# Next quad's branch announced before this quad's gather; x copied in the gather's column order; extra code of one pass and a loop

## The chip, the cores and the metric

The kernel runs on one core of a Trainium2 chip. The metric is the device time of one execution in microseconds (us); the kernel before has a median of 1836.73 us in three runs, from 1834.0 to 1844.76. TensorE (PE) multiplies matrices; its weight loads are listed as PEld. VectorE is DVE, ScalarE is ACT, GpSimd is POOL, and SyncE (SP) issues most DMA transfers. A "q" behind an engine's name (PEq, PEldq) means its sequencer.

## The reference

The reference is a network of two blocks on 256 tokens with 1024 features, all in fp32. The first block has two layers, each of a mixer of four attentions, a cross attention to a memory, and a mixture of experts (MoE), with a layer norm behind each. The second block (four layers of pooling, neighbourhood attention and convolution) is not touched. The change lies in the MoE:

```
def one_sequence(xs):
    g_logits = (xs @ w_group + b_group).astype(jnp.float32)
    g_idx = jnp.argmax(g_logits, axis=-1)
    ...
    e_logits = e_logits[jnp.arange(s), g_idx]
    top_val, top_idx = lax.top_k(e_logits, TOP_K_IN_GROUP)
    top_w = jax.nn.softmax(top_val, axis=-1) * g_weight
    ...
    hid = jax.nn.silu(jnp.einsum('sd,edf->sef', xs, w_gate)) * jnp.einsum('sd,edf->sef', xs, w_up)
    return jnp.einsum('sef,efd->sd', hid * gates[:, :, None], w_down)
```

There are 32 experts in 8 groups of 4. A token goes to one group and to two experts in it. An expert has a gate and an up matrix (1024 x 256 each) and a down matrix (256 x 1024), so each is 1 MiB.

## The kernel before

The program is written by a class `Net`. Its parts are coroutines that a planner, `Flow`, interleaves; the order of the instructions on each engine is thus fixed when the program is written. `moe(l)` writes the MoE of layer l (0 or 1). It walks over eight **quads** q, one per group of four experts. An expert has 32 places for tokens, so a quad has 128 places in one pass. If more than 32 tokens choose one expert, the quad takes further passes; their number, `more`, is known only at run time, and stands in a register.

The x of a layer (two tiles of 128 tokens x 1024) is written by `ln_affine` (L1104 multiplies by the gain, L1105 adds the bias, in place). For each tile the four pieces of 512 columns are shared between POOL (tile 0) and DVE (tile 1). DVE does the router's small operations behind that, from L1322 on.

For quad q the steps on PE are these:

- `gather` (the product at L1400): x is multiplied by the one-hot matrix `disp` to collect the quad's tokens, transposed. The weights that PE loads are columns k, k+8, k+16, ... of x, with k from 0 to 7, thus 128 columns at a stride of 8 elements. One gather is 16 products in fp32; the trace shows each as two loads and two matmuls, so one gather is 32 of each. `disp` is the name in the trace for the main pass; in the extra passes, and in the first gather of a layer, it is named `y`.
- `gate_up`: 128 rows in the trace `ps<-w,xg` with the expert weights that SP has loaded.
- The branch `up{l}_{q}` (L1533): if `more > 1`, the code of the extra passes runs (dispatch, gather, gate_up); otherwise PE jumps over it. Two passes are written out (the second behind a test at L1536), and from the fourth pass on a loop runs (L1538 and L1539).
- The gather of quad q+1, the matrices of `combine_mats`, and `down` with the quad's down weights into `acc`.
- The branch `down{l}_{q}` (L1584), with extra passes in the same form (tests at L1587 and L1589).

Two hints (`mark_branch_hint_location`, in the trace `BRANCH_PREFETCH_HINT` of L2345, on PE alone) name a branch ahead of time. The hint for `down{l}_{q}` stands right behind the up extras, and the hint for `up{l}_{q+1}` right behind the down extras, just ahead of the gate_up of quad q+1. The hint for quad 0 stands in front of the first gather.

At the end of the layer L1608 computes `x * ALPHA + acc` on DVE in four pieces.

Of the kernel before, what the change touches and what calls it, by code (L numbers as in the profile page):

```python
# [14 lines left out]
OP = mybir.AluOpType  # L15
AX = mybir.AxisListType

P = 128
# [5 lines left out]
ALPHA = 4.0 ** 0.25  # L24
# [111 lines left out]
class Net:  # L136
# [958 lines left out]

        self.flow.spawn(gen(), 0)

    def ln_affine(self, rows, eng=None):

        for tb in range(2):  # L1100
            for nh in range(2):
                e = eng[2 * tb + nh] if eng else self.nc.gpsimd
                x = self.x[tb][:, nh * 512:nh * 512 + 512]
                e.tensor_tensor(x, x, rows[0][nh], OP.mult)  # L1104
                e.tensor_tensor(x, x, rows[1][nh], OP.add)  # L1105

    def trans_bank(self, xs, j):

# [197 lines left out]
    def router(self, l, wr, rb):  # L1306

        nc = self.nc
        xf = [self.M2("xf32") for _ in range(4)]
        yield 0, 4.0  # L1310
        for j in range(4):
            self.affine_t(xf[j], self.trans_bank(self.halves(self.x), j), j,
                          lambda k: self.col("ln_mem_g", 8 * l + k), lambda k: self.col("ln_mem_b", 8 * l + k))
            yield 0.6, 0
        self.ln_affine(self.rows, (nc.gpsimd, nc.gpsimd, nc.vector, nc.vector))
        yield 0, 0.8
        p = self.ps()
        for tb in range(2):
# [25 lines left out]
        p = self.ps()  # L1344
# [47 lines left out]
    def gather(self, d, xg):  # L1392

        res = []
        dv = d.rearrange("p t e s -> p t (e s)")
        for k0 in range(0, 8, 4):
            p = self.ps()
            for j in range(4):
                for tb in range(2):
                    self.mm(p[:, j * P:(j + 1) * P], self.x[tb][:, k0 + j::8], dv[:, tb, :], tb == 0 and j == 0, tb == 1)  # L1400
            t = xg[k0 // 4].rearrange("p (k s) -> p k s", k=4)
            if k0:
                self.nc.vector.tensor_copy(xg[1], p)  # L1403
            else:
                self.nc.scalar.copy(xg[0], p)
            res += [t[:, j, :] for j in range(4)]
        return res
# [68 lines left out]
    def moe(self, l):  # L1476
        nc, tc = self.nc, self.tc
# [7 lines left out]
        hx = self.e("hx", [P, EXTRA * 256])  # L1485
# [3 lines left out]
        h, h2 = self.places()  # L1489
# [3 lines left out]
        mores = nc.values_load_multi_w_load_instructions(nri[0:1, :], min_val=0, max_val=8)[1]  # L1493
        pe = [mybir.EngineType.PE]
# [18 lines left out]
        for q in range(8):  # L1513
            if q == 1 and l == 0:
                prep = self.flow.spawn(self.band(), 0)
            wg = [self.raw("E", "expert_w_gate", l, 4 * q + j, 8) for j in range(4)]
            wu = [self.raw("E", "expert_w_up", l, 4 * q + j, 8) for j in range(4)]
            gv, uv = [w for w, _ in wg], [w for w, _ in wu]
            more = mores[q]
            rk = self.s("rk", [P, 2, 4], bufs=1)  # L1520
            if q:
                h, h2 = self.places()

            def extra_up(out):
                nc.vector.tensor_scalar(rk, rk, -32.0, None, OP.add)
                self.gate_up(self.gather(self.dispatch(rk, onehot(h2)), [self.y(0), self.y(1)]), gv, uv, out)

            gates = gates or rest()
            now, d0 = comb, d
            if q < 7:  # L1530
                d = self.dispatch(rank[:, :, 4 * q + 4:4 * q + 8])
            self.gate_up(xg, gv, uv, h)
            with tc.If(more > 1, label=f"up{l}_{q}"):  # L1533
                nc.vector.tensor_copy(rk, rank[:, :, 4 * q:4 * q + 4])
                extra_up(hx[:, 0:256])
                with tc.If(more > 2):  # L1536
                    extra_up(hx[:, 256:512])
                    with tc.If(more > 3):  # L1538
                        with tc.For_i(3, more) as i:  # L1539
                            extra_up(h2)  # L1540
                            nc.vector.tensor_copy(hx[:, self.at(i)], h2)
            tc.mark_branch_hint_location(f"down{l}_{q}", more > 1, pe)
            for _, i in wg + wu:
                self.used(i)
            if q == 3:
                self.far.close()
                if l:
                    self.near.close()
                    assert self.plan is None or not self.live_p
                self.other(split=SPLITS, more=MORE[l])  # L1550
                if l:
                    self.perm, self.capp = self.near.enter_context(self.tc.tile_pool(name="late", bufs=LATE, reuse_waits="tile", side="right")), LATE
                self.keep, self.stage = True, 2 * l + 1
                self.n_split = SPLITS
                self.pump()
                main.lane = "ps"
            yield 8.5, 0
            yield from between(3 * q)
            if q < 7:
                xg = self.gather(d, xt)  # L1560
                now = now or self.combine_mats(flat(d0), gates[:, :, 0, :])
                comb = self.combine_mats(flat(d), gates[:, :, q + 1, :])
                ht = self.down_in(h)
                yield 5.0, 0 if q > 2 else 3.0
                yield from between(3 * q + 1)
            else:
                ht = self.down_in(h)
            if q == 7 and not l:
                self.adas.append(self.flow.spawn(self.ada(1), 2, 6.0))
            gq = gates[:, :, q, :]  # L1570
            wd = [self.raw("E", "expert_w_down", l, 4 * q + j, 2) for j in range(4)]
            dv = [w for w, _ in wd]

            def extra_down(h, src=None):
                dx, h2 = self.places()
                if h is None:
                    h = h2
                    nc.vector.tensor_copy(h, src)
                nc.vector.tensor_scalar(rk, rk, -32.0, None, OP.add)
                d2 = self.dispatch(rk, onehot(dx))  # L1580
                self.down(self.down_in(h), dv, *self.combine_mats(flat(d2), gq, "x"))

            def extras():
                with tc.If(more > 1, label=f"down{l}_{q}"):  # L1584
                    nc.vector.tensor_copy(rk, rank[:, :, 4 * q:4 * q + 4])
                    extra_down(hx[:, 0:256])
                    with tc.If(more > 2):  # L1587
                        extra_down(hx[:, 256:512])
                        with tc.If(more > 3):  # L1589
                            with tc.For_i(3, more) as i:  # L1590
                                extra_down(None, hx[:, self.at(i)])

            self.down(ht, dv, *now, q == 0)
            extras()
            if q < 7:
                tc.mark_branch_hint_location(f"up{l}_{q + 1}", mores[q + 1] > 1, pe)
            if q == 7:
                nc.scalar.preload_act_table_set("natural_log_exp_and_others")
            for _, i in wd:
                self.used(i)  # L1600
            if q == 7:
                self._ahead()
            if q == 7:
                st = [self.s("bn", [P, 2, 6], bufs=2) for _ in range(2)]
                for half in range(2):
                    for tb in range(2):
                        x = self.x[tb][:, half * 512:half * 512 + 512]
                        nc.vector.scalar_tensor_tensor(x, x, ALPHA, self.acc[tb][half], OP.mult, OP.add)  # L1608
                        self.bn_half(st, half, tb)
            yield 6.0, 0 if q > 2 else 10.0  # L1610
            yield from between(3 * q + 2)
            if q == 2 and l == 0:
                yield prep.done
# [530 lines left out]
    def layer_b(self, l):  # L2144

        with ExitStack() as ctx:
            self.phase(ctx, 6)
            self.stage = 2 * l
            self.other(ring2=RING2)
            self.exp = ctx.enter_context(self.tc.tile_pool(name="exp", bufs=1, reuse_waits="tile"))  # L2150
            self.y = lambda i, dt=F32: self.e(f"y{i}", [P, 512], dt)
            self.rows = [[], []]
            for i in range(4):
                t, c = self.y(i), i % 2 * 512
                self.nc.sync.dma_start(t, self.a["ln_mem" + ("_g", "_b")[i // 2]][l:l + 1, c:c + 512].to_broadcast([P, 512]))
                self.rows[i // 2].append(t)
            self.wr = self.router_weights(l)
            self.pump()
            yield from self.moe(l)

# [188 lines left out]
```

## Time and profile before

| | |
|---|---|
| median of 3 runs | 1836.73 us |
| profiled execution, its own time | 1837.78 us |
| its span, first to last instruction | 1836.0 us |
| mean granted clock of TensorE | 0.947 of full speed |
| PE busy | 1649.1 us, 90% |
| DVE busy | 918.4 us, 50% |
| MoE of layer 0, of layer 1 | from about 306 to 602 us, from 876 to 1250 us |

The page of the profile lists busy times and the chain of work that ended last; the grouped list says how long instructions of one kind took; the timeline shows them in order; the view of one source line shows a branch's wait on each engine's sequencer; the table of windows shows how busy the DMA engines were in a stretch.

### The profile page before, as it was taken

The page shows a single profiled execution, that of the slowest core. Times are in us where ns is not written, and L with a number is a line of the kernel's source. Part 1 is how long each engine was busy: PE and PEld are TensorE (multiplying, and loading weights), DVE is VectorE, ACT ScalarE, POOL GpSimd, SP SyncE. Part 2 cuts the span into 40 slices and gives each one's busy share as a digit, 9 for nine tenths or more (in the row PEclk, how much of TensorE's full clock was granted, in tenths as well). Part 3 has the DMA queues.
Part 4 walks back from the last instruction along what each step waited for, and adds up shares of the span by engine and source line. Part 5 has one row for each costly group of instructions (what it writes and reads, how often), then busy time and mean ns, then how long its engine had stood idle before and what let it go on. Part 6 is the DMA issues. An engine that isn't in the chain of part 4 may idle for free. (4 is left out here: it accounts for less than half of the span.)

```text
span 1836.0 us, 29061 instructions
## 1 busy us (share of the span) xinstructions
PE 1649.1 (90%) x11357; PEld 1297.9 (71%) x11357; DVE 918.4 (50%) x2160; ACT 701.1 (38%) x1422; POOL 165.9 (9%) x248
## 2 busy tenths in 40 slices
PE   7999997788888799988898898997998999899997
PEld 6767985556765466686656675866887886699785
DVE  5567545252112756766121243247555566576645
ACT  4654540102212355442010132234545565455543
POOL 4000201000000300031000000002001112000101
PEclk9999998899999899999899999998998999999999
DMA  8266557989957955576357497897456866385630
GB/s 306 85 204 229 187 206 302 389 327 416 364 197 310 385 164 183 184 285 255 129 223 329 168 412 301 317 364 280 139 188 135 207 97 84 121 293 171 235 111 24
DMA packets 145964, 427.29 MB, mean 233 GB/s; under 512 B 12252, under 2 KB 19652, under 8 KB 121172
## 3 DMA queue, kind: packets, MB, share of 16 engines
q1 hardware_dynamic: 140660, 411.19, 60.6%
q0 software_dynamic: 5088, 13.32, 5.3%
q8 instruction: 124, 2.03, 0.5%
q14 instruction: 92, 0.75, 0.1%
HBM read 423.43 MB, written 1.05 MB: 231 GB/s over the span
## 5 line engine op out<-in xcount | busy, mean ns | idle before, releaser
L308 DVE TENSOR_TENSOR wlo<-w,whi 128x512 fp32r<-128x512 f32 (+2 forms) x586 | 395.4, 709 | 265.0 <-ACT whi L307 262.8
L307 ACT CAST whi<-w 128x512 fp32r<-128x512 f32 (+2 forms) x592 | 341.5, 611 | 249.6 <-PE ps L366 199.1
L366 PE MATMUL ps<-xth,whi 128*128 128x256 f32 x896 | 263.9, 295 | 8.7 <-ACT whi L307 5.2
L366 PE MATMUL ps<-xth,wlo 128*128 128x256 f32 x896 | 259.3, 289 | 4.4 <-DVE wlo L308 4.4
L366 PE MATMUL ps<-xtl,whi 128*128 128x256 f32 x896 | 258.5, 289 | 0.6 <-DVE xtl L1142 0.4
L366 PE MATMUL ps<-whi,xth 128*128 128x512 f32 (+2 forms) x512 | 206.6, 404 | 4.4 <-ACT whi L307 4.0
L366 PE MATMUL ps<-wlo,xth 128*128 128x512 f32 (+2 forms) x512 | 198.8, 388 | 0.2 <-DVE wlo L308 0.2
L366 PE MATMUL ps<-whi,xtl 128*128 128x512 f32 (+2 forms) x512 | 198.6, 388 | 0.2 <-DVE xtl L1142 0.2
L366 PEld LDWEIGHTS ps<-xth,whi 128*128 128x128 f32 x896 | 176.0, 196 | 18.1 <-ACT whi L307 12.8
L366 PEld LDWEIGHTS ps<-xth,wlo 128*128 128x128 f32 x896 | 174.8, 195 | 5.2 <-DVE wlo L308 5.2
L366 PEld LDWEIGHTS ps<-xtl,whi 128*128 128x128 f32 x896 | 175.2, 196 | 3.2 <-issue 1.4
L366 PEld LDWEIGHTS ps<-whi,xth 128*128 128x128 f32 x512 | 99.0, 193 | 33.2 <-ACT whi L307 6.6
L366 PEld LDWEIGHTS ps<-whi,xtl 128*128 128x128 f32 x512 | 98.4, 192 | 20.7 <-DVE xtl L1142 0.9
L366 PEld LDWEIGHTS ps<-wlo,xth 128*128 128x128 f32 x512 | 98.9, 193 | 18.3 <-DVE wlo L308 1.3
L366 PE MATMUL ps<-disp,x 128*128 128x128 f32 x384 | 94.4, 414 | 15.7 <-PEq L1533 6.8
L366 PEld LDWEIGHTS ps<-disp,x 128*128 128x128 f32 x384 | 93.0, 336 | 19.0 <-issue 14.3
L366 PE MATMUL ps<-w,xg 128*32 128x256 f32 x1536 | 86.9, 382 | 6.1 <-issue 2.8
L366 PE MATMUL ps<-w,y 128*32 128x512 f32 (+1 forms) x784 | 80.9, 551 | 6.9 <-DVE y L1451 4.4
L366 PEld LDWEIGHTS ps<-w,xg 128*32 128x32 f32 x1536 | 52.1, 111 | 40.2 <-issue 7.3
L1142 POOL TENSOR_TENSOR xtl<-aff,xth 128x512 fp32r<-128x512 f32 x9 | 11.6, 1285 | 696.9 <-ACT xth L1141 521.5
L1403 DVE COPY xg<-ps 128x512 f32<-128x512 f32 x14 | 9.7, 692 | 118.9 <-PE ps L366 118.9
L1435 DVE TENSOR_TENSOR y<-y,ps 128x256 f32<-128x256 f32 x12 | 5.1, 421 | 112.6 <-ACTq L1533 62.9
(516 smaller groups left out, 2567.0 us busy)
## 6 DMA issues: line engine op xcount, KB each, us to landing
w<-in_expert_w_gate_dram SPq DMA_DIRECT2D x64, 1024.0 KB, 14.4
w<-in_expert_w_up_dram SPq DMA_DIRECT2D x64, 1024.0 KB, 12.6
w<-in_expert_w_down_dram SPq DMA_DIRECT2D x64, 1024.0 KB, 10.0
w<-in_ada_w_dram SPq DMA_DIRECT2D x48, 1024.0 KB, 6.1
w<-in_pool_w_in_dram SPq DMA_DIRECT2D x24, 1024.0 KB, 10.9
w<-in_na_w_in_dram SPq DMA_DIRECT2D x24, 1024.0 KB, 6.5
w<-in_w_in_dram SPq DMA_DIRECT2D x16, 1024.0 KB, 11.5
w<-in_conv_w_in_dram SPq DMA_DIRECT2D x16, 1024.0 KB, 6.0
```

What stands on the lines that cost most here:

```text
L307: self.nc.scalar.copy(hi, src)
L308: (self.nc.gpsimd if self.spare and k % 2 else self.nc.vector).tensor_tensor(lo, src, hi.bitcast(F32), OP.subtract)
L366: self.nc.tensor.matmul(out, lhsT, rhs, start=start, stop=stop, skip_group_check=True)
L1142: (nc.gpsimd if j == 2 else nc.vector).tensor_tensor(lo, fs[j - 1], hi.bitcast(F32), OP.subtract)
L1403: self.nc.vector.tensor_copy(xg[1], p)
L1435: nc.vector.tensor_tensor(h, sg, p[:, 256:512], OP.mult)
```

## The change

- `ln_affine` writes the sum of L1104's product and the bias to two further tiles, `xp`, of [128, 8, 128]: `xp[:, k, j]` is column 8j + k of x. For this the second operation reads x and the bias in order and writes with the order turned round. `x` itself then holds only the product.
- `gather` loads `xp[tb][:, k0 + j, :]`, 128 columns that lie next to each other.
- L1608 reads `xp` in the turned order and writes x in plain order.
- The hint for `up{l}_{q+1}` stands right behind the up extras of quad q, so the gather of quad q+1, the `down` of quad q and the branch of its down extras lie between it and the branch it names. The hint for `down{l}_{q}` is dropped. The hint for quad 0 stays.
- Of the extra passes one is written out; from the third pass on (`more > 2`) the loop runs.
- The scratch space for POOL's DMA descriptors is set to 8192.

```
-    def ln_affine(self, rows, eng=None):
+    def ln_affine(self, rows, eng=None, xp=None):
...
                 e.tensor_tensor(x, x, rows[0][nh], OP.mult)
-                e.tensor_tensor(x, x, rows[1][nh], OP.add)
+                o, b = x, rows[1][nh]
+                if xp:
+                    o = xp[tb].rearrange("p k j -> p j k")[:, nh * 64:nh * 64 + 64, :]
+                    x, b = (v.rearrange("p (j k) -> p j k", k=8) for v in (x, b))
+                e.tensor_tensor(o, x, b, OP.add)
...
-                    self.mm(p[:, j * P:(j + 1) * P], self.x[tb][:, k0 + j::8], dv[:, tb, :], tb == 0 and j == 0, tb == 1)
+                    self.mm(p[:, j * P:(j + 1) * P], self.xp[tb][:, k0 + j, :], dv[:, tb, :], tb == 0 and j == 0, tb == 1)
...
                 extra_up(hx[:, 0:256])
                 with tc.If(more > 2):
-                    extra_up(hx[:, 256:512])
-                    with tc.If(more > 3):
-                        with tc.For_i(3, more) as i:
-                            extra_up(h2)
-                            nc.vector.tensor_copy(hx[:, self.at(i)], h2)
-            tc.mark_branch_hint_location(f"down{l}_{q}", more > 1, pe)
+                    with tc.For_i(2, more) as i:
+                        extra_up(h2)
+                        nc.vector.tensor_copy(hx[:, self.at(i)], h2)
+            if q < 7:
+                tc.mark_branch_hint_location(f"up{l}_{q + 1}", mores[q + 1] > 1, pe)
...
-                with tc.If(more > 1, label=f"down{l}_{q}"):
+                with tc.If(more > 1):
                     nc.vector.tensor_copy(rk, rank[:, :, 4 * q:4 * q + 4])
                     extra_down(hx[:, 0:256])
                     with tc.If(more > 2):
-                        extra_down(hx[:, 256:512])
-                        with tc.If(more > 3):
-                            with tc.For_i(3, more) as i:
-                                extra_down(None, hx[:, self.at(i)])
+                        with tc.For_i(2, more) as i:
+                            extra_down(None, hx[:, self.at(i)])
...
-            if q < 7:
-                tc.mark_branch_hint_location(f"up{l}_{q + 1}", mores[q + 1] > 1, pe)
...
-                        x = self.x[tb][:, half * 512:half * 512 + 512]
-                        nc.vector.scalar_tensor_tensor(x, x, ALPHA, self.acc[tb][half], OP.mult, OP.add)
+                        x = self.x[tb][:, half * 512:half * 512 + 512].rearrange("p (j k) -> p j k", k=8)
+                        xp = self.xp[tb].rearrange("p k j -> p j k")[:, half * 64:half * 64 + 64, :]
+                        acc = self.acc[tb][half].rearrange("p (j k) -> p j k", k=8)
+                        nc.vector.scalar_tensor_tensor(x, xp, ALPHA, acc, OP.mult, OP.add)
...
+            self.xp = [self.e(f"xp{tb}", [P, 8, P]) for tb in range(2)]
...
-    nc = _bacc.Bacc("TRN2", target_bir_lowering=False, num_devices=1)
+    nc = _bacc.Bacc("TRN2", target_bir_lowering=False, num_devices=1, dynamic_dma_scratch_size=8192)
```

The changed program numbers its lines a little higher: the up branch L1533 becomes L1537, its inner test L1536 becomes L1540, the loop L1541; the down branch L1584 becomes L1587, its inner test L1590; L1105 becomes L1109, L1608 becomes L1609.

The order of PE's instructions moves at two places of each quad. The first is the end of quad 0's up extras in layer 0, where PE comes out of the branch and begins the gather of quad 1. Before:

```order
L1536 UNCONDITIONAL_BRANCH
L1533 UNCONDITIONAL_BRANCH
L1542 REGISTER_ALU
L2345 BRANCH_PREFETCH_HINT
L366 MATMUL ps<-disp,x 128x128 x8
L366 MATMUL pl<-disp,x 128x128 x8
L369 MATMUL ps<-ident,y_3124 128x128 x2
```

The hint of L2345 here names the down branch of the same quad. With the change, at the same place:

```order
L1540 UNCONDITIONAL_BRANCH
L1537 UNCONDITIONAL_BRANCH
L1545 REGISTER_ALU
L2347 BRANCH_PREFETCH_HINT
L366 MATMUL pl<-disp,xp_2966 128x128
L366 MATMUL pl<-disp,xp_2967 128x128
```

The hint now names the up branch of quad 1, and the gather's weights come from `xp` (the last two rows stand four times in turn for each of `pl` and `ps`).

The second place is the end of quad 0's down extras, where the gate_up of quad 1 begins. Before:

```order
L1589 UNCONDITIONAL_BRANCH
L1587 UNCONDITIONAL_BRANCH
L1584 UNCONDITIONAL_BRANCH
L1596 REGISTER_ALU
L2345 BRANCH_PREFETCH_HINT
L366 MATMUL pl<-w_2974,xg 32x256
```

The hint here names the up branch of quad 1, which stands behind this gate_up. With the change:

```order
L1591 UNCONDITIONAL_BRANCH
L1590 UNCONDITIONAL_BRANCH
L1587 UNCONDITIONAL_BRANCH
L366 MATMUL ps<-w_2976,xg 32x256
L366 MATMUL ps<-w_2978,xg 32x256
```

No hint stands there any more. Counted in the instructions that the trace shows (two loads and two matmuls per product), an up branch before jumped over 994 PE instructions and now over 670, a down branch over 321 and now over 222, and the inner up test L1536 over 674.

## Rows read from the trace of the kernel before

**Rows 1.** The page: chain of work that ended last, share of the span by engine.

```profile
PE 25%; DVE 3%; ACT 1%; DMA 1%; issue 1%; POOL 0%; ACTq 0%; DVEq 0%; POOLq 0%
```

**Rows 2.** Grouped list, 285 to 1250 us: count | busy us, mean ns | idle before.

```profile
L366 PEld LDWEIGHTS ps<-disp,x 128*128 128x128 f32 x384 | 93.0, 336 | 19.0 <-issue 14.3 <-ACTq L1533 4.6
...
L366 PEld LDWEIGHTS ps<-y,x 128*128 128x128 f32 x112 | 27.2, 335 | 8.3 <-issue 8.3
...
L366 PEld LDWEIGHTS pl<-y,x 128*128 128x128 f32 x80 | 19.5, 335 | 6.6 <-issue 6.6
...
L366 PEld LDWEIGHTS pl<-disp,x 128*128 128x128 f32 x64 | 15.7, 334 | 10.0 <-issue 6.8 <-ACTq L1533 1.6 <-ACTq L1538 1.6
...
L366 PEld LDWEIGHTS ps<-wr,xf 128*128 128x128 f32 x64 | 7.3, 192 | 0.0
...
L366 PEld LDWEIGHTS pl<-band,pu 128*128 128x128 f32 x48 | 5.6, 191 | 1.7 <-issue 1.7
```

**Rows 3.** Timeline, 318 to 345 us: the gather of quad 1 (start, length, engine).

```profile
323.47 3.88 PEld L366 LDWEIGHTS ps<-disp,x 128*128 128x128 f32 x16 [2.89 <-ACTq L1533]
...
327.25 3.94 PEld L366 LDWEIGHTS pl<-disp,x 128*128 128x128 f32 x16
```

**Rows 4.** Table of windows; last columns: PE clock, DMA busy share, GB/s.

```profile
310.00:330.00 20.00, 17.56 (x173) 14.41 (x173) 3.21 (x15) 3.61 (x9) 0.00 (x0) 0.87 0.68 263
...
390.00:410.00 20.00, 16.62 (x189) 10.70 (x187) 4.99 (x17) 2.13 (x4) 0.54 (x1) 0.99 0.66 244
410.00:460.00 50.00, 44.32 (x344) 36.03 (x344) 12.48 (x25) 10.28 (x19) 0.00 (x0) 0.90 1.01 411
...
890.00:930.00 40.00, 34.34 (x361) 27.27 (x350) 3.97 (x12) 3.60 (x6) 0.00 (x0) 0.91 0.08 29
...
1000.00:1050.00 50.00, 41.85 (x409) 29.21 (x409) 10.54 (x38) 8.76 (x20) 0.00 (x0) 0.94 0.32 118
1050.00:1110.00 60.00, 57.66 (x444) 46.85 (x446) 19.52 (x36) 20.14 (x37) 3.36 (x5) 0.98 1.02 406
```

**Rows 5.** Timeline of PE: gate_up of layer 0 quad 4, layer 1 quad 1.

```profile
429.20 7.39 PE L366 MATMUL ps<-w,xg 128*32 128x256 f32 x128
...
958.60 7.11 PE L366 MATMUL ps<-w,xg 128*32 128x256 f32 x128 [0.73 <-PEq L1589]
```

**Rows 6.** View of L1533 (up branch), PE's sequencer, six stretches: ns min/median/max.

```profile
L1533 PEldq COMPARE_BRANCH  x3: 1678/2604/5817, 319.6 to 381.1; - x3
...
L1533 PEldq COMPARE_BRANCH  x2: 2812/3125/3438, 405.8 to 434.9; - x2
...
L1533 PEldq COMPARE_BRANCH  x3: 89/4453/4938, 474.1 to 587.0; - x3
...
L1533 PEldq COMPARE_BRANCH  x3: 89/89/967, 889.9 to 992.1; - x3
...
L1533 PEldq COMPARE_BRANCH  x2: 739/2148/3557, 1043.5 to 1082.9; - x2
...
L1533 PEldq COMPARE_BRANCH  x3: 359/1699/2221, 1132.4 to 1232.3; - x3
```

**Rows 7.** Views of L1536 and L1587 (inner tests, no hint), PE's sequencer.

```profile
L1536 PEldq COMPARE_BRANCH  x5: 75/197/3404, 542.0 to 1012.5; - x5
...
L1587 PEldq COMPARE_BRANCH  x5: 65/187/349, 579.7 to 1037.3; - x5
```

**Rows 8.** Views of L2345 (hints), 1150 to 1198 us, and L1533, 1190 to 1198 us.

```profile
L2345 PEldq BRANCH_PREFETCH_HINT  x2: 35/35/35, 1174.0 to 1196.3; - x2
...
L1533 PEldq COMPARE_BRANCH  x1: 1699/1699/1699, 1194.3 to 1194.3; - x1
```

**Rows 9.** Timeline of DVE, 283 to 316 us: adds at L1105 (start, length).

```profile
293.74 1.64 DVE L1105 TENSOR_TENSOR x<-x,y 128x512 f32<-128x512 f32 x1
...
297.08 0.69 DVE L1105 TENSOR_TENSOR x<-x,y 128x512 f32<-128x512 f32 x1
```

**Rows 10.** Grouped list, 285 to 1250 us: L1608.

```profile
L1608 DVE SCALAR_TENSOR_TENSOR x<-x,acc 128x512 f32<-128x512 f32 x4 | 2.7, 674 | 1.1 <-PEq L1584 1.1
```

More of the change, by code (lines that the diff above doesn't have):

```diff
@@ L1314, in router @@
             yield 0.6, 0
-        self.ln_affine(self.rows, (nc.gpsimd, nc.gpsimd, nc.vector, nc.vector))
+        self.ln_affine(self.rows, (nc.gpsimd, nc.gpsimd, nc.vector, nc.vector), self.xp)
         yield 0, 0.8
```

## The prediction

> **What bounds the kernel now.** I read the page first. In the chain that ended last PE holds 25% of the span and no other engine more than 3% [rows 1], and PE is busy for 90% of the span; so time taken off PE is time won, unless what PE works on comes too late. The grouped list then shows what the touched steps cost on PE, and that the rows of one shape differ by a factor of two [rows 2]. The timeline shows that a gather is bounded by its weight loads, which follow each other without a hole [rows 3]. The table of windows tells where the expert weights already come as fast as the DMA engines move them [rows 4], and the timeline of PE where PE uses them as they land [rows 5]. The views of the branches give the waits on PE's sequencer [rows 6 to 8]. The sum is made against the profiled execution, 1837.8 us, which is 1.05 us above the median.
>
> **1. The gather's loads: -80.5 us.** The four groups with x as weights hold 384 + 112 + 80 + 64 = 640 loads and 93.0 + 27.2 + 19.5 + 15.7 = 155.4 us [rows 2]: 243 ns for each load. A gather has 32, so these are 20 gathers: 16 main ones and 4 in extra passes. One of them runs from 323.47 to 331.19 us, 7.7 us for 32 loads [rows 3]. The same shape, 128x128 fp32, taken from columns that lie side by side, costs 7.3 / 64 = 114 ns (`ps<-wr,xf`) and 5.6 / 48 = 117 ns (`pl<-band,pu`) [rows 2]. With `xp` the gather's columns lie side by side, so I take 117 ns: 640 x 0.117 = 74.9 us, 80.5 less, or 4.0 us for each gather. PE goes from the gather to `down` to the next gate_up with little idle time, so all of it is on the path. The Trainium skill ("SBUF — State Buffer", section on the DMA port swizzle, its note on cachelines) says that accesses are at full speed only if at least two fall into one line of 16 bytes, which a stride of 8 fp32 misses; for the loads the rows agree, and the sum is the same by either.
>
> **2. What the weights give back: +14 us.** PE can gain only what the transfers allow. In layer 0 the DMA engines are busy at 1.01 from 410 to 460 us, and in this stretch the gate_up of quad 4 takes 7.39 us where another takes 7.11 [rows 4, 5]: there the weights land as they are used. Five gathers lie ahead of that place, 5 x 4.0 = 20 us. To come 20 us earlier the transfers have only the free shares of two holes, 0.32 x 20 = 6.4 us at 310 to 330 and 0.34 x 20 = 6.8 us at 390 to 410 [rows 4], 13.2 us at most. So 6.8 us are lost if both close fully and 20 if neither does; I take 10, nearer to the first, because the holes come from buffers that come free late, and PE will free them earlier. In layer 1 the shares are 0.08 at 890 to 930 us and 0.32 at 1000 to 1050 [rows 4]: 36.8 + 34 us free, more than its 11 gathers x 4.0 = 44 us. Only the stretch from 1050 us at 1.02 is full, with one gather at its beginning: 4 us. The sum is 14. Bounds: 0, and 40 if all of layer 0's nine gathers (36 us) and this one are lost.
>
> **3. Up branches: -10 us.** Thirteen of the 16 up branches are taken, and the six rows hold their waits: 10.1 + 6.25 + 9.4 + 1.0 + 4.3 + 4.3 = 35.3 us [rows 6] (the three that go on into an extra pass wait 0.09). If the earlier hint hides all but the shortest of these, 0.36 us, 13 x 0.36 = 4.7 stays: -30.6. Against that stands the branch at 1194.3 us: its hint came at 1174.0, 20.3 us ahead, and PE still waited 1.70 us [rows 8]. So lead alone is not enough, and the other bound is 0. I take a third of the way: eight of the thirteen waits are longer than this 1.70 us, by 16.2 us in sum, and of that I count 10 as won. A wait that gets longer is a rival below.
>
> **4. Down branches without a hint: 0 us.** The inner test L1587 skips about as many instructions as the down branch will (some 220), has no hint, and waits 0.35 us at most [rows 7]. That is no more than a hinted down branch costs.
>
> **5. One pass and a loop: +6 us.** Four extra ups and downs run. Quad 0 of layer 1 has three passes and goes through the loop once in up and once in down where it had straight code. The loop adds a copy and two jumps on each side. Lower bound 1 us (two short copies). Above: two misses as long as the longest up wait, 5.8 each [rows 6], and a few us of loop code, 15 us. I take two misses near 3 us, as the unhinted L1536 has at most 3.4 [rows 7]. The two quads with two passes still test and skip the second; 670 instructions less one body make this no dearer.
>
> **6. Turned writes and reads: +4 us.** The adds that now write `xp` stand on DVE ahead of the router's operations, and they took 1.64 and 0.69 us [rows 9]; L1608 takes four times 0.67 us per layer [rows 10] with the next norm behind it. No row shows fp32 written at a stride of 512 bytes. If nothing changes it is 0; if DVE slows down by the factor of the weight loads (243 / 117 = 2.1) it is about 1.1 x (2.33 + 2.7) x 2 layers = 11 us. I take 4, since a slower DVE pays at the short adds, but those of 1.64 us are already held up by POOL, and may hide part. POOL's adds have room before the first gather. Beside this: by the Trainium skill's note named in step 1 the stride of 512 bytes also misses the line; an estimate by it is the upper end, 7 us more than in my sum. No run here shows it yet.
>
> **7. The smaller scratch: 0 us.** POOL issues few transfers in this kernel, and none of them is on the path.
>
> **Sum.** -80.5 + 14 - 10 + 6 + 4 = -66.5: 1837.8 - 66.5 = 1771.3 for a profiled execution, 1770 on the scale of the median.
>
> **The rivals.**
> - **B, all branches hidden (0.20).** The hint a quad ahead hides the up waits: term 3 becomes -30.6, the others stay: 1837.8 - 87.1 = 1750.7, about 1750. For it: the waits are longest where transfers are full, as if the fetch only came too late. Against it: the 20 us of rows 8.
> - **C, the weights become the bound (0.14).** Term 2 is 40: 1837.8 - 40.5 = 1797.3, about 1796. For it: the stretch from 410 to 460 us is full already [rows 4]. Against it: layer 1 has holes of more than 70 us.
> - **D, slower: the hint is lost and branches miss (0.05).** Between the hint and its branch stands another taken branch, the down branch. If that one uses up the hint or drives the fetched code out, and itself misses, 13 up and 13 down branches wait as the worst now, 5.8 us [rows 6]: 26 x 5.8 = 151 us in place of 35.3 and about 7 for the downs, +109. With the other terms (-56.5) that is 1837.8 + 52 = 1890. It ends on the slow side when the mean of the 26 waits is above (42 + 56.5) / 26 = 3.8 us. Against it: unhinted tests wait 3.4 us for 674 instructions and 0.35 for some 220 [rows 7], which would make 13 x 3.4 + 13 x 0.35 = 49 us, +7, and a time near 1787. The Trainium skill ("Runtime: NRT & Kernel Launch", section "Instruction fetch mechanics") says that a taken branch whose target is not in the current window of two pages (256 instructions each) waits for a fetch. By it the up skip of 670 misses without a hint and the down skip of 222 mostly does not; rows 7 agree in kind.
> - **E, the copy does nothing for the loads (0.03).** If the loads of a gather are slow for another reason than their stride (both matmul operands of the quick rows differ too), -80.5 and +14 fall away: 1837.8 + 0 = about 1837. Against it: four groups at 335 ns each and two at 191 of the same shape [rows 2].
>
> **How the numbers follow.** My forecast has 0.58, B 0.20, C 0.14, D 0.05, E 0.03. The predicted time is 1770. A change of under 0.5% (9 us) is about what a measurement of this kernel can't tell from none. Forecast, B and C are faster by more: 0.92; E is the same: 0.03; D is slower: 0.05. The range reaches from B with a little less given back by the weights (1750 less 10) to C and a little above: 1740 to 1800. D and E stay outside, and some of the edges of B and C, together less than 2 in 10.
>
> **What would show it.** The loads of `xp` at 110 to 125 ns each (their duration near 190 in place of 335), a gather in about 3.8 us; the up branch's waits between 5 and 35 us in sum, and the down branch's at 0.2 to 0.5 us each; the gate_ups of layer 0 from quad 3 on with idle time that ends on a DMA of expert weights, 10 us or so; L1609 and L1109 with a mean between 0.67 and 1.4 us. The prediction is wrong if the loads stay above 200 ns, if up waits grow beyond 50 us, or if PE waits for weights for more than 30 us.

## The result, and the profile after

The changed kernel takes 1785.21 us (median of 4 runs, 1781.82 to 1790.64) against 1840.74 us of the kernel before in the same comparison: ratio 0.9703, 95% interval 0.9656 to 0.9749. It is 55.5 us faster, where 66.5 were predicted, and lies inside the range (1740 to 1800). The total was nearly right; several of its terms were not: one had the wrong sign, and one counted a gain that is not there.

The page of the profile after (busy time by engine; chain by engine):

```profile
PE 1590.7 (89%) x11357; PEld 1234.5 (69%) x11357; DVE 926.4 (52%) x2162; ACT 702.5 (39%) x1422; POOL 165.2 (9%) x248
...
PE 23%; DVE 4%; DMA 3%; ACT 1%; issue 1%; POOL 1%; ACTq 0%; DVEq 0%; POOLq 0%
```

PE lost 58 us of busy time, and its count of matmuls is the same as before, 11357: the same products run, in the same order. So the k-th weight load of one trace can be set beside the k-th of the other, and the difference of their starts shows where time was won. Up to the last gate_up of layer 1 these differences add up to 64.7 us won in the 20 gathers, 8.7 lost in the gate_ups with the up branches behind them, and 6.5 lost in all the rest; 2.4 more are lost after it. That makes 47 us, the difference of the two spans (1836.0 and 1788.8 us).

The grouped list after, 285 to 1250 us, answers to [rows 2, 10]:

```profile
L366 PEld LDWEIGHTS ps<-disp,xp 128*128 128x128 f32 x384 | 49.0, 209 | 23.3 <-issue 20.0 <-ACTq L1540 1.6 <-ACTq L1537 1.6
...
L366 PEld LDWEIGHTS ps<-y,xp 128*128 128x128 f32 x112 | 16.8, 239 | 8.3 <-issue 8.3
...
L366 PEld LDWEIGHTS pl<-y,xp 128*128 128x128 f32 x80 | 10.9, 219 | 6.9 <-issue 6.9
L366 PEld LDWEIGHTS pl<-disp,xp 128*128 128x128 f32 x64 | 10.5, 254 | 11.0 <-issue 8.1 <-ACTq L1537 2.9
...
L1609 DVE SCALAR_TENSOR_TENSOR x<-xp,acc 128x512 f32<-128x512 f32 x8 | 8.4, 1045 | 1.1 <-PEq L1587 1.1
...
L1109 DVE TENSOR_TENSOR xp<-x,y 128x512 f32<-128x512 f32 x4 | 6.0, 1506 | 0.1
```

The 640 loads are busy for 49.0 + 16.8 + 10.9 + 10.5 = 87.2 us, 136 ns each, where 117 were predicted. The final multiply-add takes 1.05 us against 0.67 [rows 10], the add 1.51 against a mean of 1.16 before (4.7 us for four in the same list); the prediction had named 0.67 to 1.4 for both.

Why 136 and not 117 shows when the gathers are put beside the granted clock. The timeline of weight loads before, and the table of windows before (last three columns: PE clock, DMA share, GB/s):

```profile
306.11 3.91 PEld L366 LDWEIGHTS ps<-y,x 128*128 128x128 f32 x16 [2.73 <-issue]
...
356.43 1.26 PEld L366 LDWEIGHTS pl<-disp,x 128*128 128x128 f32 x5 [1.49 <-issue]
...
383.92 3.88 PEld L366 LDWEIGHTS pl<-disp,x 128*128 128x128 f32 x16 [1.65 <-ACTq L1533]
```
```profile
306.00:310.00 4.00, 3.86 (x16) 3.90 (x17) 0.00 (x0) 0.00 (x0) 0.54 (x2) 0.50 1.05 424
...
384.00:387.70 3.70, 3.70 (x16) 3.70 (x16) 2.83 (x10) 0.00 (x0) 1.42 (x5) 0.90 0.96 372
```

The same two views after:

```profile
310.76 1.87 PEld L366 LDWEIGHTS pl<-y,xp 128*128 128x128 f32 x16
...
352.43 0.71 PEld L366 LDWEIGHTS pl<-disp,xp 128*128 128x128 f32 x3 [2.54 <-issue]
353.03 3.53 PEld L366 LDWEIGHTS ps<-disp,xp 128*128 128x128 f32 x16
...
403.29 3.65 PEld L366 LDWEIGHTS ps<-disp,xp 128*128 128x128 f32 x32 [2.32 <-issue]
```
```profile
310.80:312.60 1.80, 1.80 (x19) 1.80 (x17) 0.00 (x0) 0.59 (x1) 0.00 (x0) 1.00 1.03 396
...
353.00:356.50 3.50, 3.50 (x19) 3.50 (x18) 0.00 (x0) 0.59 (x1) 0.00 (x0) 0.50 1.03 426
```

Before, 16 loads took 3.9 us whether the granted clock was 0.50 (the level of 1.2 GHz) or 0.90. After, they take 1.87 us at 1.00 and 3.53 at 0.50. A gather at the lower clock therefore wins little. That of quad 2 in layer 0, which comes behind a branch wait of 6.1 us, is busy for 7.0 us against 7.8, and the idle time inside it, 2.54 us against 1.49, takes this back: it won no time at all. Six of the 20 gathers after run at the lower clock in part or whole and are busy for 5.0 to 7.0 us each; the other fourteen take 3.65 to 3.73, as the gather at 403.29.

The up branch after (L1537, in six stretches of the same order as [rows 6]) and the down branch:

```profile
L1537 PEldq COMPARE_BRANCH  x3: 2417/3901/6076, 318.4 to 374.8; - x3
...
L1537 PEldq COMPARE_BRANCH  x3: 341/2771/2835, 400.0 to 465.7; - x3
...
L1537 PEldq COMPARE_BRANCH  x2: 70/1644/3217, 509.4 to 561.3; - x2
...
L1537 PEldq COMPARE_BRANCH  x3: 70/82/6427, 873.2 to 964.9; - x3
...
L1537 PEldq COMPARE_BRANCH  x3: 358/363/3877, 1006.7 to 1090.0; - x3
...
L1537 PEldq COMPARE_BRANCH  x2: 348/834/1321, 1148.3 to 1183.4; - x2
...
L1587 PEldq COMPARE_BRANCH  x16: 93/352/450, 333.6 to 1200.3; - x16
```

The thirteen taken up branches wait 34.3 us in sum, against 35.3. The hint a quad ahead has hidden nothing in sum. The down branches, now without a hint, wait 0.45 us at most.

Where the weights hold PE up is seen in the timeline of PE, at the gate_ups of quad 4 of layer 0 and of quad 4 of layer 1:

```profile
418.57 1.50 PE L366 MATMUL ps<-w,xg 128*32 128x256 f32 x23
420.74 2.79 PE L366 MATMUL ps<-w,xg 128*32 128x256 f32 x45 [0.67 <-issue]
423.97 0.62 PE L366 MATMUL ps<-w,xg 128*32 128x256 f32 x2 [0.44 <-DMA w<-in_expert_w_up_dram]
426.74 5.21 PE L366 MATMUL ps<-w,xg 128*32 128x256 f32 x58 [2.15 <-DMA w<-in_expert_w_up_dram]
...
1036.52 4.11 PE L366 MATMUL ps<-w,xg 128*32 128x256 f32 x70
1042.61 3.64 PE L366 MATMUL ps<-w,xg 128*32 128x256 f32 x58 [1.98 <-DMA w<-in_expert_w_up_dram]
```

The first takes 431.95 - 418.57 = 13.4 us against 7.39 [rows 5], the second 9.7 against the 7.1 of a gate_up without a wait. So the weights give back 8.6 us: 6.0 and 2.6. Of the 6.0 only 3.3 are idle time; the rest is slower matmuls behind it, at a mean granted clock of 0.69: the last 58 take 5.21 us, where 58 at 1.00 take 3.64 in the second.

Last, the layer 1 mixer, which the change does not touch. It runs the same 1355 matmuls between about the same two points in both kernels (windows, before and after):

```profile
612.00:876.00 264.00, 236.37 (x1355) 179.35 (x1355) 174.38 (x431) 118.47 (x279) 40.26 (x37) 0.94 0.67 237
```
```profile
589.00:861.00 272.00, 242.97 (x1355) 184.54 (x1355) 174.06 (x430) 116.98 (x274) 38.38 (x35) 0.90 0.64 227
```

PE is busy 6.6 us longer with the same work at a mean clock of 0.90 instead of 0.94, and the stretch is 8 us longer. Whether this belongs to the change is taken up below.

### The profile page after: what moved, and what is told of

Same layout as the page of the kernel before. It is cut to its first block, busy times and chain, and to the rows that moved or that the text cites. A ratio compares the mean times of both kernels' runs of the same rounds, so it can differ in the third digit from the quotient of the medians.

```text
span 1788.8 us, 29185 instructions
## 1 busy us (share of the span) xinstructions
PE 1590.7 (89%) x11357; PEld 1234.5 (69%) x11357; DVE 926.4 (52%) x2162; ACT 702.5 (39%) x1422; POOL 165.2 (9%) x248
## 3 DMA queue, kind: packets, MB, share of 16 engines
q8 instruction: 117, 1.92, 0.4%
HBM read 423.43 MB, written 1.05 MB: 237 GB/s over the span
## 5 line engine op out<-in xcount | busy, mean ns | idle before, releaser
L366 PE MATMUL ps<-xth,whi 128*128 128x256 f32 x896 | 263.0, 293 | 10.5 <-ACT whi L307 5.4
L366 PEld LDWEIGHTS ps<-whi,xth 128*128 128x128 f32 x512 | 99.4, 194 | 32.8 <-ACT whi L307 6.6
L366 PE MATMUL ps<-w,xg 128*32 128x256 f32 x1536 | 91.1, 388 | 10.5 <-DMA w<-in_expert_w_up_dram 5.6
L366 PE MATMUL ps<-disp,xp 128*128 128x128 f32 x384 | 50.8, 295 | 19.6 <-PEq L1537 10.3
L366 PEld LDWEIGHTS ps<-disp,xp 128*128 128x128 f32 x384 | 49.0, 209 | 23.3 <-issue 20.0
L366 PEld LDWEIGHTS ps<-w,y 128*32 128x32 f32 x784 | 25.5, 114 | 52.1 <-issue 37.4
## 6 DMA issues: line engine op xcount, KB each, us to landing
w<-in_expert_w_down_dram SPq DMA_DIRECT2D x64, 1024.0 KB, 10.9
```

Of the source, the lines that this page charges most:

```text
L366: self.nc.tensor.matmul(out, lhsT, rhs, start=start, stop=stop, skip_group_check=True)
```

## The experiments

Each kernel was timed beside the kernel before. This was done in three groups, each on another chip; the kernel before has a median of 1840.16 us beside e1 to e4, 1843.84 beside e5 to e8 and 1840.75 beside e9 to e12. Kernels of different groups are therefore best compared by their ratios to it. Executions of one kernel spread by 3 to 22 us.

| kernel | copy | code | up hint | median us | ratio, 95% interval |
|---|---|---|---|---|---|
| changed | by add | short | early | 1785.21 | 0.9703 (0.9656 to 0.9749) |
| e11, changed again | by add | short | early | 1789.11 | 0.9713 (0.9689 to 0.9736) |
| e1 | by add | long | late, down too | 1794.78 | 0.9753 (0.9722 to 0.9784) |
| e2 | none | short | early | 1832.19 | 0.9956 (0.9935 to 0.9978) |
| e3 | by add | short | late, down too | 1779.24 | 0.9664 (0.9626 to 0.9703) |
| e4 | by add | short | none | 1814.37 | 0.9851 (0.9819 to 0.9882) |
| e5 | none | short | late, down too | 1832.92 | 0.9932 (0.9907 to 0.9957) |
| e6 | by add | loop alone | late, down too | 1820.45 | 0.9874 (0.9838 to 0.9910) |
| e7 | by ScalarE | short | late, down too | 1773.05 | 0.9611 (0.9587 to 0.9635) |
| e8 | ScalarE, stride 4 | short | late, down too | 1827.97 | 0.9907 (0.9882 to 0.9932) |
| e9 | ScalarE, stride 2 | short | late, down too | 1775.35 | 0.9651 (0.9628 to 0.9673) |
| e10 | by ScalarE | short | early and late | 1772.25 | 0.9625 (0.9602 to 0.9649) |
| e12 | by ScalarE | short | late | 1769.13 | 0.9614 (0.9585 to 0.9642) |

The branch waits on PE's sequencer, summed over all rows of each profile, and the wait of one branch, that of quad 1 in layer 1, which comes behind the three passes of quad 0:

| us | before | changed | e1 | e2 | e3 | e4 | e5 | e7 | e10 | e11 | e12 |
|---|---|---|---|---|---|---|---|---|---|---|---|
| up | 35.5 | 34.5 | 26.2 | 40.8 | 29.4 | 73.1 | 32.8 | 27.0 | 29.2 | 31.6 | 27.7 |
| down | 7.6 | 5.2 | 8.8 | 5.1 | 6.8 | 5.0 | 6.3 | 6.7 | 5.7 | 5.0 | 4.8 |
| inner tests, loops | 9.3 | 6.3 | 9.7 | 6.3 | 6.2 | 7.6 | 3.6 | 6.2 | 6.5 | 7.6 | 8.7 |
| layer 1 quad 1, up | 0.97 | 6.43 | 0.75 | 6.39 | 1.87 | 6.31 | 1.05 | 0.73 | 0.95 | 6.29 | 1.71 |

**e1, the copy alone.** Hints and extra code of the kernel before, with the copy:

```
-    self.mm(p[...], self.x[tb][:, k0 + j::8], ...)
+    self.mm(p[...], self.xp[tb][:, k0 + j, :], ...)
```

> Only the copy in the gather's order (and the scratch size it needs); hints and extra code as before. Theory 1 (the loads are the whole gain): a time within 5 us of the changed kernel, ratio to before 0.968 to 0.974, up waits about 35 us in sum. Rival (the earlier hint or the shorter code holds a part of the gain): 8 us or more slower than the changed kernel, ratio 0.975 or above.

It came out 45 us under before and 6 to 10 above the changed kernel (e11 and the first measurement), with an interval that is for the most part above theory 1's bound. So the copy brings most of the gain, and something else in the change brings a part, as far as overlapping intervals can tell. The up waits fell by 9 us here, though hints and extra code are those of before: so much they differ between two kernels by their timing alone.

**e2, hints and code alone.** The change without `xp`.

> Only the moved hints and the shorter extra code; the gather reads x at the stride of 8 as before. Theory 1: the up waits stay near 35 us in sum, the down waits fall by 2 to 3 us, the time is at most 4 us under before, ratio 0.997 to 1.001. Rival: ratio 0.995 or below, up waits of 25 us or less.

It is 8 us faster (4 to 12 by the interval), between the two, although the up waits grew to 40.8 us. All branch waits together are 52.2 us, as before (52.4), so what is gained here does not show in the branches. The two parts, 45 us (e1) and 8, add up to the 53 to 55 us of the whole change.

**e3 and e4, the hints.** e3 puts both hints back; e4 has none for the up branches:

```
-            if q < 7:
-                tc.mark_branch_hint_location(f"up{l}_{q + 1}", mores[q + 1] > 1, pe)
```

> The changed kernel with both hints back at their old places; the shorter code and the copy stay. Theory 1 (a hint starts its fetch only when PE comes near the branch, so its place a quad earlier gives nothing): the same time as the changed kernel within 5 us, up waits 28 to 40 us in sum. Rival (the early hint helps): up waits 10 us or more above the changed kernel's 34.3. Second rival (the early hint hurts, since the down branch lies between): up waits 25 us or less and a faster time.

> The changed kernel without any hint for an up branch. If hints do nothing: up waits stay at 34 us in sum and the time is the changed kernel's within 5 us. If hints bring the fetch forward in some quads (the waits of 0.34 to 0.36 us in quads 4 to 6): all thirteen skips wait 2 to 6 us, in sum 45 to 60 us, and the time is 10 to 20 us above the changed kernel's, ratio to before 0.976 to 0.982.

The up waits of e3, 29.4 us, are those of theory 1; its time is 6 us under the changed kernel, on the side of the second rival, 0.9664 against 0.9703. The intervals overlap, also with that of e11, the changed kernel measured again, which has 0.9713. Without hints the time rises by 29 us, more than was expected, and all thirteen skips wait:

```profile
L1536 PEldq COMPARE_BRANCH  x16: 70/5554/7806, 318.3 to 1200.1; - x16
```

So hints are worth 39 us of up waits, and the place a quad ahead adds nothing to that: 34.5 us with it, 29.4 with the old place. One row shows why: the up branch of layer 1 quad 1, in the changed kernel, in e4 and in e3.

```profile
L1537 PEldq COMPARE_BRANCH  x1: 6427/6427/6427, 938.5 to 938.5; - x1
```
```profile
L1536 PEldq COMPARE_BRANCH  x1: 6314/6314/6314, 942.5 to 942.5; - x1
```
```profile
L1537 PEldq COMPARE_BRANCH  x1: 1869/1869/1869, 940.4 to 940.4; - x1
```

Between the early hint and this branch PE runs quad 0's extra down passes, with the loop and the loop's own hint. There the early hint is as good as none (6.43 and 6.31 us). The other kernels with an early hint alone, e2 and e11, show 6.39 and 6.29, and the kernels with a late hint under 2 us; e6, where the loop in front of the late hint jumps back, is the exception with 6.1. Whether the loop's code or its hint displaces the early hint was not tested.

**e5, the shorter code alone**, on the kernel before.

> The kernel before with the shorter extra code alone: no copy, hints at their old places. Theory 2 (the shorter code is a gain by itself, since the same shortening came out 10 to 15 us faster beside the copy): 6 to 14 us under before, ratio 0.992 to 0.997. Rival (what was gained there came from the moved hints or from chance): ratio 0.998 to 1.002.

It is 12.5 us faster (1843.84 x 0.0068; 8 to 17 by the interval): theory 2 holds for the time. The branch waits fell, 42.8 us in sum against 52.4. The inner test L1536 shows the largest piece, the two skips of 3.3 and 3.4 us (the longer in [rows 7]) being now a shorter jump:

```profile
L1536 PEldq COMPARE_BRANCH  x5: 75/187/560, 539.3 to 1005.4; - x5
```

In most of the other kernels with the short code one of the two still waits 2.1 to 4.5 us, so this piece varies with what else is in the program. The two profiles do not place the gain: their spans are only 3.1 us apart (1836.0 and 1832.9), and e2, with the same short code, gains 8 us with no less waits. So where the shorter code saves time stays open.

**e6, the loop alone**, on e3, with no pass written out:

```
-                extra_up(hx[:, 0:256])
-                with tc.If(more > 2):
-                    with tc.For_i(2, more) as i:
-                        extra_up(h2)
-                        nc.vector.tensor_copy(hx[:, self.at(i)], h2)
+                with tc.For_i(1, more) as i:
+                    extra_up(h2)
+                    nc.vector.tensor_copy(hx[:, self.at(i)], h2)
```

> The kernel of e3 with every extra pass in the loop, none written out, so that an up branch jumps over some 340 instructions. If the length of the jump sets the wait: up waits under 15 us in sum and 8 to 20 us under e3, ratio 0.955 to 0.962. Rival (any jump that leaves the code already fetched costs the same): up waits 25 to 40 us in sum and the time of e3 within 5 us, ratio 0.964 to 0.970.

Neither: it is 41 us slower than e3 by the medians, 39 by the ratios. The up waits did not fall (41.0 us), so a jump over half as many instructions is not cheaper here. In addition this kernel runs a loop twice, in quad 0 of layer 1, and so jumps back. The timeline of PE at that place in the down extras:

```profile
931.26 0.97 PE L366 MATMUL acc<-y,ctx 128*128 128x512 f32 x3 [0.29 <-DVE y L1469]
936.78 0.70 PE L369 MATMUL ps<-ident,y 128*128 128x128 f32 x2 [4.55 <-DVE y L1578]
937.27 0.66 PE L369 MATMUL pl<-ident,y 128*128 128x128 f32 x2
937.73 0.85 PE L366 MATMUL pl<-r_el,y 128*128 128x4 f32 x4
938.51 3.48 PE L366 MATMUL ps<-w,y 128*32 128x512 f32 x16
```

PE is idle for 4.55 us, and DVE, which it waits for, sat idle for 5.22 us at the loop (L1586). The view of that line, 930 to 937 us, shows why:

```profile
L1586 SPq DRAIN  x3: 7/7/7, 935.3 to 935.6; - x3
...
L1586 PEldq EVENT_SEMAPHORE  x3: 51/51/51, 935.5 to 936.0; - x3
...
L1586 PEldq DRAIN  x2: 13/310/607, 931.7 to 935.8; - x2
```

The engines meet at the end of the loop before they jump back. PE's sequencer is there at 931.7 us and goes on at 935.5, right behind that of SyncE, the last to come, at 935.3. The 16 matmuls behind it take 3.48 us where the pass before took 1.92: the granted clock is 0.54 there against 1.00. In the change itself the loop runs once at most and never jumps back. Where the rest of e6's 41 us lies was not traced further.

**e7, the copy by ScalarE**, on e3; x stays whole:

```
+                e.tensor_tensor(x, x, rows[1][nh], OP.add)
+                if xp:
+                    self.nc.scalar.copy(xp[tb].rearrange("p k j -> p j k")[...], x.rearrange("p (j k) -> p j k", k=8))
```

> The kernel of e3 with the adds of L1105 in place in plain order, ScalarE copying x into the gather's order behind them, and L1608 reading plain x. If the turned operations of DVE lie on the path: the final multiply-adds return from 1.05 to 0.67 us each, 3 us per layer are saved, 4 to 8 us under e3, ratio 0.961 to 0.965. Rival (ScalarE's copies come too late for the first gather): the first gather starts 2 to 5 us later and the time is that of e3 or above.

The multiply-adds are back at 0.67 us, ScalarE's copies take 1.09 each:

```profile
L1107 ACT COPY xp<-x 128x512 f32<-128x512 f32 x8 | 8.0, 1087 | 5.8 <-POOL x L1105 5.8
...
L1607 DVE SCALAR_TENSOR_TENSOR x<-x,acc 128x512 f32<-128x512 f32 x8 | 5.4, 674 | 1.1 <-PEq L1585 1.1
```

It is 6 us under e3 by the medians, 10 by the ratios; the intervals touch. The turned operations of DVE explain at most 4.3 us of this, 8 x 0.37 for the multiply-adds and 4 x 0.34 for the adds. The two profiled spans (1787.2 and 1771.5 us) differ by 15.7 us, of which 6.2 lie in the layer 1 mixer and 5.7 in gathers at another clock, which e7 does not touch. So that DVE's turned operations were on the path is likely, but not shown apart from this. The first gather starts at 306.9 us, as in the changed kernel (307.6) and 1.9 later than in e3, too little to matter beside this.

**e8 and e9, the stride.** The copy with 4 or 2 columns interleaved, so that a gather's columns are 16 or 8 bytes apart:

```
+            self.xp = [self.e(f"xp{tb}", [P, 8 // s, P, s]) for tb in range(2)]
...
+                    self.mm(p[...], self.xp[tb][:, (k0 + j) // s, :, (k0 + j) % s], ...)
```

> The kernel of e7 with the copy laid out so that a gather's 128 columns lie 4 elements (16 bytes) apart. If what counts is that two elements fall into one stretch of 16 bytes: loads as slow as at a stride of 8, 240 to 245 ns, and a time near that of the kernel before, ratio 0.995 to 1.0. If loads slow down in proportion to the stride: near 150 to 180 ns. If a stride of 4 is free: 117 ns at full clock and the time of e7 within 4 us.

> The kernel of e7 with the gather's columns 2 elements (8 bytes) apart. If two elements in one stretch of 16 bytes are enough: loads as in e7 (120 ns at full clock, 1.9 us for 16), ScalarE's copies under 1.0 us, and the time of e7 within 4 us, ratio 0.958 to 0.964. Rival (every stride above 1 costs): loads of 150 to 240 ns, 15 to 55 us above e7.

At a stride of 4 the loads are as slow as at 8: 151.7 us busy for the 640, 237 ns each, of which the largest group is

```profile
L366 PEld LDWEIGHTS ps<-disp,xp 128*128 128x128 f32 x384 | 90.7, 329 | 17.2 <-issue 9.3 <-ACTq L1536 5.0 <-ACTq L1539 2.8
```

and the time is that of e5, the same kernel without a copy (0.9907 and 0.9932). At a stride of 2, 16 loads take 1.96 us at full clock against 1.86, and the copies 0.65 us against 1.09:

```profile
318.15 1.96 PEld L366 LDWEIGHTS pl<-disp,xp 128*128 128x128 f32 x16 [2.07 <-issue]
```
```profile
L1107 ACT COPY xp<-x 128x512 f32<-128x512 f32 x8 | 5.0, 649 | 7.3 <-POOL x L1105 6.5 <-DVE x L1105 0.7
```

So the price is a step between 2 and 4 elements. The cheaper copies of e9 buy nothing that shows: its median is 2 us above e7's, and 6 above that of e12, measured beside it.

**e10 and e12, both up hints or the late one alone**, without down hints, on e7.

> The kernel of e7 without down hints and with two hints for each up branch, one at the new and one at the old place. If the early hint alone loses some quads because the branches and the loop of the quad before come between (layer 1, quad 1): the late hint brings them back, up waits 22 to 30 us in sum with layer 1 quad 1 under 2 us, the time of e12 within 4 us. If the early hint does bring the fetch forward where no loop comes between: up waits 15 us or less and 8 us or more under e12.

> The changed kernel, unaltered, beside the others of this call. If the moved hints cost time: ratio 0.967 to 0.973, that is above e3's 0.966. If e3's lead was chance: ratio 0.963 to 0.967.

> The kernel of e7 with the up hints at their old place and no down hints. If a down hint is worth nothing, as the prediction said: down waits 5 to 6 us in sum as in the changed kernel, the time of e7 within 4 us, ratio 0.958 to 0.964. Rival (a down branch without a hint misses in some quads): down waits of 8 us or more and a slower time.

With the late hint added, layer 1 quad 1 waits 0.95 us, and the up waits are 29.2 and 27.7 us: the early hint adds nothing where no loop comes between either. The down branches wait 4.8 us in sum without hints. e12 is the fastest median of all, 1769 us, but not apart from e7 and e10. Against the changed kernel beside it (e11) it is 20 us, 1.1%, faster.

## Why the prediction was right, and where it was not

**Term 1, the loads (-80.5).** Right in kind and in rank, mis-sized: 64.7 us in the trace. The step that failed is the price of 117 ns for every load. It came from rows at full clock; six of the 20 gathers run at the lower clock in part or whole, where a load takes 220 ns. This makes 87.2 us of loads instead of 74.9, 12 of the 16 us that are missing. In the rows of before this could not be seen at the gather itself, because the stride hid it: 243 ns at either clock. Rival E is excluded by e8, which differs from e7 in the stride alone and loses the gain.

**Term 2, the weights (+14).** Right in kind and place, 8.6 us at the two places named or beside them, and 5 us too high.

**Term 3, the early hint (-10).** Wrong. The doubt named there, the 20 us of lead that did not help [rows 8], was the true reading, and should have set the term to 0 or above. Moving the hints alone won nothing and seems to cost time: from e5 to e2 the up waits grow by 8 us and the time by 4 (0.9932 to 0.9956), from e3 to e11 the up waits by 2 and the time by 9 (0.9664 to 0.9713); in both pairs the intervals overlap. Rival D had the mechanism, in one place instead of 26: of the 8 us, 5 are the branch behind the loop, where the hint is lost. That the down branch between uses up every hint, as rival D had it, is excluded: quads 4 to 6 of layer 1, with a taken down branch between and no loop, wait 0.35 to 0.36 us in the changed kernel. Rival B falls with the 34.3 us of up waits that are left, and rival C with term 2.

**Term 4, down hints (0).** Right: 7.6 us with hints, 5.2 without, and 4.8 in e12. [rows 7] had shown it. The Trainium skill ("Runtime: NRT & Kernel Launch", "Instruction fetch mechanics") says that a taken branch whose target lies outside the two pages of code at hand waits for a fetch; the trace agrees in kind, with 0.45 us at most for skips of 222 instructions without a hint and 3.46 us at least for those of 670 (e4).

**Term 5, one pass and a loop (+6).** Wrong sign: -12.5 (e5), by a mechanism that is in the main open. The prediction priced the loop entry and counted the shortened skips at nothing, though [rows 7] held a wait of 3.4 us, and the trace a second of 3.3, that such a cut could shorten. The loop's test and entry cost 0.2 us a piece in the changed kernel's profile.

**Term 6, the turned operations (+4).** Right as far as the rows show: the two operations take DVE 4.3 us longer. The multiply-add grew by a factor of 1.55, not by the 2.1 that was tried from the loads. The 6 to 10 us from e3 to e7 are more than that, and what lies beyond was not separated from the clock.

**Not in the sum:** the layer 1 mixer, 8 us longer in the changed kernel. It is not shown to be a cost of the change. The same 1355 matmuls take 264 to 267 us in seven of the fourteen profiles (before, e1, e4, e5, e7, e8, e12; mean granted clock 0.92 to 0.94) and 270 to 272 us in the other seven (both of the changed kernel, e2, e3, e6, e9, e10; 0.90 to 0.91). e1, the copy alone, and e2, hints and code alone:

```profile
595.00:860.00 265.00, 235.83 (x1355) 179.66 (x1355) 172.91 (x430) 116.65 (x274) 38.29 (x35) 0.93 0.65 232
```
```profile
609.00:879.00 270.00, 244.53 (x1356) 185.69 (x1356) 173.75 (x430) 118.47 (x279) 39.74 (x37) 0.90 0.66 234
```

So the copy does not bring the lower clock, and no single part of the change goes with it: e3 and e7 have the same hints and the same short code and stand on different sides. What decides it stays open; it moves a single profile by some 6 us.

So the total came out near because errors cancelled, and that is luck. Terms 3 to 5 were put at -4 in sum, and e2, which holds them alone, is 8 us faster; but behind this stand a gain of 10 that did not come and a cost of 6 that was a gain of 12.5. Terms 1, 2 and 6 were put at -62.5, and e1 is 45 us faster (40 to 51 by the interval): term 1 lost 16 us of it, term 2 gave back 5, and 6 more are not placed by any row.

## What to carry to other kernels

The load that was slow for its stride was as slow at either clock; once mended, its price followed the clock. So price a mended form at the clock of its own stretch, not at the clock of the row that it is taken from. A hint was worth much here, but not for its lead: put it behind any loop that comes ahead of the branch, and look in the trace whether it worked (in e6 it did not). When a rearranged copy is wanted, try the engine that is idle just then, and leave the operands of the others in plain order: e7, e10 and e12 are the fastest kernels here. And when two profiles differ, look first at the stretches that the change does not touch.

## What the runs showed of the hardware that was not expected

- fp32 weight loads of 128x128: 117 ns at a stride of 1, 122 at 2 (1.96 us for 16), 237 at 4 and 243 at 8. The last was 3.9 us for 16 at granted clocks of 0.50 and 0.90 alike.
- A branch hint ahead of a loop that then ran was worth nothing at the one branch where this happens (6.3 to 6.4 us of wait with it, 6.3 without).
- At a loop's jump back PE was idle for 4.55 us and DVE for 5.22, since the engines meet there and SyncE's sequencer came last (e6).
